# A fixed order for the prologue and the first eight weight units of a two-layer decoder trunk

## The chip, the cores and the metric

The kernel runs on one core of one Trainium2 chip. The metric is the device time of one execution in microseconds; less is better. It is given as the median of three executions, and a profile shows one more execution.

## What is computed

The reference is a decoder trunk of two layers on 256 positions of width 1024, all in float32. Each layer is a SwiGLU block, a mixer (Mamba-2 in the first layer, block-sparse attention in the second) and another SwiGLU block. Each of these six blocks works on a modulated norm of x, whose shift, scale and gate come from a product of SiLU(c) with a 1024 x 3072 matrix:

```python
def rmsnorm(x, g):
    y = xf * lax.rsqrt(jnp.mean(xf * xf, axis=-1, keepdims=True) + RMS_EPS)
    return (y * g).astype(x.dtype)

def modulate(x, g, c_act, w, b):
    m = c_act @ w + b
    shift, scale, gate = jnp.split(m, 3, axis=-1)
    return rmsnorm(x, g) * (1.0 + scale[:, None, :]) + shift[:, None, :], gate[:, None, :]

def swiglu(h, w_gate, w_up, w_down):
    return (jax.nn.silu(h @ w_gate) * (h @ w_up)) @ w_down

for i in range(DEPTH):
    h, g = modulate(x, norm_g[i, 0], c_act, mod_w[i, 0], mod_b[i, 0])
    x = x + 0.5 * g * swiglu(h, ffn_w_gate[i, 0], ffn_w_up[i, 0], ffn_w_down[i, 0])
    ...
```

## The kernel before

The weights stream through the core once. They are cut into units of 16 blocks of 128x128 (1 MB). A unit lands in one of three buffers `raw`, and is split into two halves of eight blocks. Of each half, ScalarE makes the high part (`hi`, a rounded copy, L309) and VectorE the low part (`lo`, raw minus `hi`, L316); there are six buffers of each, so three units. X, the modulated input, is split in the same way into XH and XL. TensorE then makes three matmuls of 256 columns per block (`prod`, L382 to L384): hi with XH, hi with XL, lo with XH. A unit is 48 matmuls.

The modulation vectors are made on VectorE. A block of 128 columns of the modulation matrix (`mraw`, 512 KB, five buffers) is multiplied by c, spread over all partitions in `cb`, and summed (`modulation`, L340); a small operation makes the vector's column of it (`vectors`, L325 and L327).

The prologue (L991 to L1025) loads c, the identity and x, spreads c over the partitions by eight transposes (L1011), squares x and adds the squares (L1014 to L1016), sums them over partitions by 16 instructions on TensorE (`rstd_sum`, L393), takes the root (L396) and makes the row `rb` (L406 to L408). The first eight units are the part of the first SwiGLU block that goes row block by row block: unit k needs only row block k of X. For each k VectorE makes two sums (scale block k, L327, and shift block k, L325), then u = x * scale * rb (L1032); ScalarE makes XH of it (L1035), VectorE XL (L1036). So unit k can begin as soon as its own two sums are there. All eight PSUM banks collect these eight units (L535 to L545). From unit 8 on a unit holds all row blocks of one output column, and its results are evacuated as they come.

The order of loads is a list (`LOADS`): for each of the first units scale block, shift block, weights. SP issues them in this order; `issue` (L272) goes on as long as a buffer of the list's next item is free, by the program's own count, and each load waits on the chip for the instruction that last reads its buffer. `pump` (L351) writes out splits and sums in the order of `ORDER`. In the prologue (`manual_schedule`) the program's order is kept; after it a scheduler sets the order of each engine's queue, by the buffers' dependencies and its own estimates. An engine works off its queue in order.

Of the kernel before, what the change touches and what calls it, by code (L numbers as in the profile page):

```python
# [146 lines left out]
def stream_order():  # L147


    items = []  # L150
    for j in range(6):
        for d in range(NK):
            items.append((j, 16 + d))
            if j < 5:
                items.append((j + 1, 8 + d))
        if j < 5:
            items += [(j + 1, d) for d in range(NK)]
    at = []
    for first, last, count in WINDOWS:
        at += [first + (last - first) * n / count for n in range(count)]  # L160
    assert len(at) == len(items) == 128
    order = []
    n = 0
    for i in range(len(ALL_UNITS)):
        if i < NK:
            order += [("m", 0, 8 + i)] * (i < 2) + [("m", 0, i)] + [("m", 0, 9 + i)] * (1 <= i < NK - 1)
        order.append(("w", i))
        while n < len(items) and at[n] <= i + 1:
            order.append(("m",) + items[n])
            n += 1  # L170
    assert n == len(items)
    return order
# [15 lines left out]
    pass  # L188


@with_exitstack
def hybrid_trunk(ctx, tc, w, mod, xt, vec, const, out, dbg=None):
    nc = tc.nc
    pool = ctx.enter_context(tc.tile_pool(name="main", bufs=1))
    psp = ctx.enter_context(tc.tile_pool(name="psum", bufs=1, space=bass.MemoryType.PSUM))
    mm, act, dve, gps = nc.tensor, nc.scalar, nc.vector, nc.gpsimd

    raw = [pool.tile([128, UW], F32, name=f"raw{i}") for i in range(N_RAW)]
    hi = [pool.tile([128, 128 * SUB], F32R, name=f"hi{i}") for i in range(N_SUB)]
# [12 lines left out]
    osel = pool.tile([128, 32], F32, name="osel")  # L212
    sel = pool.tile([128, 32], F32R, name="sel")
    b1 = pool.tile([128, 48], F32, name="b1")
    MV = pool.tile([128, 6, 3, NK], F32, name="MV")
    acc = pool.tile([128, 6, 24], F32, name="acc")
    ssq = pool.tile([128, L], F32, name="ssq")
# [8 lines left out]
    st = Core()  # L226
    st.bank = 0
    st.ut = 0
    st.sq = 0
# [32 lines left out]

    st.d = st.p = st.m = st.mdma = st.w = st.wdma = st.s = 0
    st.cur = -1
    st.on_mod = None
    st.sub = None
    st.known = set()
    st.hook = st.pending = None
    st.u = {}
    st.ahead = 2  # L270

    def issue(last=len(LOADS)):  # L272
# [32 lines left out]
    def split(q):  # L305
        i, half = SUBS[q]
        wd = 128 * SUB
        r, h, l = raw[i % N_RAW][:, half * wd:half * wd + wd], hi[q % N_SUB], lo[q % N_SUB]
        act.activation(h, r, AF.Copy)  # L309
        if st.pending:  # L310
            st.pending()
            st.pending = None
        c = wd * POOL_PART[PHASE_OF[i]] // 16
        if c:
            gps.tensor_sub(l[:, :c], r[:, :c], h[:, :c].bitcast(F32))
        ins = dve.tensor_sub(l[:, c:wd], r[:, c:wd], h[:, c:wd].bitcast(F32)).ins  # L316
        if i >= NK:
            st.sub = ins

    def vectors(j, kind, k0, k1):  # L320

        o, a = MV[:, j, kind, k0:k1], acc[:, j, 8 * kind + k0:8 * kind + k1]
        c = V_MB + 32 * j + 8 * kind
        if kind == 0:
            dve.tensor_add(o, a, V[:, c + k0:c + k1])  # L325
        elif kind == 1 and k1 == k0 + 1:
            dve.tensor_scalar(o, a, b1[:, 8 * j + k0:8 * j + k1], V[:, V_NG + 32 * j + k0:V_NG + 32 * j + k1],  # L327
                              op0=OP.add, op1=OP.mult)
# [6 lines left out]
        st.known |= {(j, 8 * kind + k) for k in range(k0, k1)}  # L335

    def modulation(j, c):
        kind, k = divmod(c, 8)
        one = j == 0 and kind < 2
        ins = dve.scalar_tensor_tensor(junk, mraw[SLOT["m", j, c]], 1.0, cb, op0=OP.mult, op1=OP.mult,  # L340
                                       accum_out=acc[:, j, c:c + 1]).ins
# [3 lines left out]
        st.m += 1  # L345
        if one or k == 7:
            vectors(j, kind, k if one else 0, k + 1)
        if st.on_mod:
            st.on_mod(j, c)

    def pump(q):  # L351

# [27 lines left out]
    def prod(ps, i, b, xh, xl, start, stop):  # L380
# [2 lines left out]
        mm.matmul(ps, h, xl, start=False, stop=False, skip_group_check=True)  # L383
        mm.matmul(ps, l, xh, start=False, stop=stop, skip_group_check=True)  # L384


    def rstd_sum(parts, n):

        ps = bank()
        c = (D, D_IN).index(n)  # L390
        for e, s in enumerate(parts):
            for t in range(2):
                mm.matmul(ps[:, t:t + 1], s[:, 128 * t:128 * t + 128], ones[:, c:c + 1], start=e == 0 and t == 0,  # L393
                          stop=e == len(parts) - 1, skip_group_check=True)
        q, r, t = (sm[:, 2 * i:2 * i + 2] for i in range(3))
        act.activation(q, ps[:, 0:2], AF.Sqrt, bias=eps)  # L396
# [104 lines left out]
    def ffn(j, p):  # L501
        i0 = BASE[p]
        with tc.tile_pool(name=f"ffn{p}", bufs=1) as fp:
# [30 lines left out]

            if p == 0:  # L535
                bs = [bank_pair() for _ in range(4)]
                for k in range(NK):
                    if k == 4:
                        preload(AF.Silu)
                    for m in range(8):  # L540
                        for s in range(2):
                            prod(bs[m // 2][:, m % 2, L * s:L * s + L], k, 2 * m + s, XH[:, k, :L], XL[:, k, :L],
                                 k == 0 and s == 0, k == NK - 1)
                        if k == NK - 1 and m % 2:
                            evac(m - 1, bs[m // 2])  # L545
                st.on_mod = None
# [444 lines left out]
    with tc.tile_pool(name="start", bufs=1) as sp:  # L991
        sq0 = sp.tile([128, NK, L], F32, name="sq0")
        ca = sp.tile([128, 8], F32, name="ca")
        xv = x.rearrange("p a b -> p (a b)")
        early = ExitStack()
# [29 lines left out]
    st.p = 2  # L1025

    def first_x(j, c):

        k = c % 8
        if c >= 8:  # L1030
            st.u[k] = utmp()
            dve.scalar_tensor_tensor(st.u[k], x[:, k, :], MV[:, j, 1, k:k + 1], rb, op0=OP.mult, op1=OP.mult)  # L1032
        else:
            S, u = MV[:, j, 0, k:k + 1], st.u[k]
            act.activation(XH[:, k, :L], u, AF.Identity, bias=S)  # L1035
            st.pending = lambda: dve.scalar_tensor_tensor(  # L1036
                XL[:, k, :L], u, S, XH[:, k, :L].bitcast(F32), op0=OP.add, op1=OP.subtract)

    first_x(0, 8)
    first_x(0, 0)  # L1040
    st.on_mod = first_x
    pump(0)
    early.close()
    ffn(0, 0)
    mamba(1, 1)
    ffn(2, 2)
# [90 lines left out]
```

## Time and profile before

| | us |
|---|---|
| median of three executions | 1115.83 (1115.04 to 1116.04) |
| the profiled execution | 1115.07 |
| its span, first to last instruction | 1113.3 |
| TensorE busy in it | 1090.7 |
| VectorE busy | 897.4 |
| ScalarE busy | 602.4 |

The rows further below come from this one execution. Its span is 1.8 us shorter than its time. A row of a timeline gives the start in us from the span's start, then the duration, then engine, line, operation and tiles. Matmuls are pipelined: one that is shown with 0.28 us begins 0.12 us after the one ahead of it. The share of the granted clock is recorded only from its first change on, so a stretch ahead of that prints as 1.00 whatever the clock was; the distance of the matmuls tells the level there.

### The profile page before, as it was taken

How to read it: one execution, taken by the hardware profiler on the slowest of the kernel's cores; microseconds unless marked ns; L12 is line 12 of the kernel's file. 1: busy time of each engine (PE TensorE's matmuls, PEld its weight loads, DVE VectorE, ACT ScalarE, POOL GpSimd, SP SyncE). 2: the span in 40 equal slices, each digit the busy share in tenths (PEclk: the TensorE clock that was granted, in tenths of full speed). 3: DMA queues.
4: the chain of work that ended last, by engine and by line, in shares of the span. 5: the costliest groups of instructions: out<-in, count | busy, mean ns of one | idle time of the engine just before them, and what ended most of it. 6: DMA issues, size and time to landing. Idle time of an engine off the chain costs nothing.

```text
span 1113.3 us, 22076 instructions
## 1 busy us (share of the span) xinstructions
PE 1090.7 (98%) x9050; PEld 1067.7 (96%) x9050; DVE 897.4 (81%) x1445; ACT 602.4 (54%) x919; POOL 55.4 (5%) x61
## 2 busy tenths in 40 slices
PE   6999999999999998999999999999999999999997
PEld 6999999999899998999999999999988899999996
DVE  6998989899899999999976889886697779555542
ACT  4463445676776657444544644454475666444541
POOL 0000001000000001000001000001211210000010
PEclk9999999999999999999999999999999999999998
DMA  9989988853444663899966499986544336555531
GB/s 349 381 335 369 352 319 302 301 200 117 175 166 142 240 238 128 302 356 367 375 246 246 160 346 334 356 308 263 186 174 156 121 115 222 190 184 183 186 136 39
DMA packets 50358, 269.00 MB, mean 242 GB/s; under 512 B 5840, under 2 KB 6608, under 8 KB 28624
## 3 DMA queue, kind: packets, MB, share of 16 engines
q1 hardware_dynamic: 50256, 267.58, 65.4%
q8 instruction: 71, 1.16, 0.4%
q14 instruction: 31, 0.25, 0.1%
HBM read 266.51 MB, written 1.05 MB: 240 GB/s over the span
## 4 chain that ended last, share of the span: by engine, by line
PE 94%; DVE 4%; ACT 1%; issue 1%; DMA 0%; SPq 0%; DVEq 0%; ACTq 0%
PE bank L383 29%; PE bank L382 29%; PE bank L384 29%; PE bank L734 1%; DVE lo L316 1%; PE bank L957 1%; PE bank L959 1%; PE bank L958 1%; PE bank L874 1%; PE bank L393 1%; PE bank L915 1%; DVE x L458 0%; ACT hi L309 0%; DMA x<-in_xt_dram 0%; DVE X L439 0%
## 5 line engine op out<-in xcount | busy, mean ns | idle before, releaser
L316 DVE TENSOR_TENSOR lo<-raw,hi 128x1024 fp32r<-128x1024 f32 x361 | 437.7, 1221 | 136.9 <-ACT hi L309 136.6
L309 ACT ACTIVATE hi<-raw 128x1024 fp32r<-128x1024 f32 x361 | 376.8, 1057 | 310.8 <-PE bank L383 253.2
L383 PE MATMUL bank<-X,hi 128*128 128x256 f32 (+1 forms) x1928 | 542.7, 282 | 1.5 <-DVE X L439 1.4
L382 PE MATMUL bank<-X,hi 128*128 128x256 f32 (+1 forms) x1928 | 538.3, 282 | 4.0 <-ACT hi L309 2.5
L384 PE MATMUL bank<-X,lo 128*128 128x256 f32 (+1 forms) x1928 | 538.8, 281 | 0.2 <-DVE lo L316 0.2
L382 PEld LDWEIGHTS bank<-X,hi 128*128 128x128 f32 x1928 | 364.2, 190 | 8.6 <-issue 3.4
L383 PEld LDWEIGHTS bank<-X,hi 128*128 128x128 f32 x1928 | 363.7, 189 | 2.8 <-DVE X L439 1.8
L384 PEld LDWEIGHTS bank<-X,lo 128*128 128x128 f32 x1928 | 363.4, 189 | 0.4 <-DVE lo L316 0.4
L384 PE MATMUL bank<-H,lo 128*128 128x256 f32 x704 | 196.9, 280 | 0.0
L382 PE MATMUL bank<-H,hi 128*128 128x256 f32 x704 | 196.3, 279 | 0.0
L383 PE MATMUL bank<-H,hi 128*128 128x256 f32 x704 | 196.2, 279 | 0.0
L340 DVE SCALAR_TENSOR_TENSOR junk<-mraw,cb 128x1024 bf16<-128x1024 f32 x144 | 175.4, 1218 | 0.9 <-DMA mraw<-in_mod_dram 0.2
L383 PEld LDWEIGHTS bank<-H,hi 128*128 128x128 f32 x704 | 132.3, 188 | 0.0
L384 PEld LDWEIGHTS bank<-H,lo 128*128 128x128 f32 x704 | 132.1, 188 | 0.0
L382 PEld LDWEIGHTS bank<-H,hi 128*128 128x128 f32 x704 | 131.6, 187 | 0.0
L416 POOL TENSOR_TENSOR ssq<-ssq,sq 128x256 f32<-128x256 f32 x36 | 34.4, 955 | 966.3 <-ACT sq L414 965.8
L522 ACT ACTIVATE sg<-bank 128x512 f32<-128x512 f32 x41 | 24.0, 585 | 38.9 <-PE bank L384 38.9
L634 DVE SCALAR_TENSOR_TENSOR cv<-bank,V,cv 128x255 f32<-128x255 f32 (+2 forms) x96 | 44.3, 474 | 0.5
L458 DVE SCALAR_TENSOR_TENSOR x<-bank,MV,x 128x256 f32<-128x256 f32 x40 | 19.1, 480 | 29.2 <-PE bank L384 29.1
L414 ACT ACTIVATE sq<-x 128x256 f32<-128x256 f32 x36 | 14.9, 414 | 50.6 <-DVE x L458 45.9
L382 PE MATMUL bank<-GH,hi 128*128 128x256 f32 x128 | 36.2, 284 | 1.1 <-DVE cv L634 0.9
L384 PE MATMUL bank<-GH,lo 128*128 128x256 f32 x128 | 36.0, 282 | 0.0
(179 smaller groups left out, 924.1 us busy)
## 6 DMA issues: line engine op xcount, KB each, us to landing
raw<-in_w_dram SPq DMA_DIRECT2D x169, 1024.0 KB, 5.1
mraw<-in_mod_dram SPq DMA_DIRECT2D x144, 512.0 KB, 6.5
raw<-in_w_dram SPq DMA_DIRECT2D x23, 512.0 KB, 8.1
x<-in_xt_dram SPq DMA_DIRECT2D x2, 512.0 KB, 4.6
out_dram<-x SPq DMA_DIRECT2D x3, 256.0 KB, 2.3
out_dram<-x SPq DMA_DIRECT2D x2, 128.0 KB, 1.9
V<-in_vec_dram SPq DMA_DIRECT2D x1, 196.5 KB, 8.3
mask<-in_const_dram SPq DMA_DIRECT2D x1, 192.0 KB, 8.1
```

The source lines that it names most:

```text
L309: act.activation(h, r, AF.Copy)
L316: ins = dve.tensor_sub(l[:, c:wd], r[:, c:wd], h[:, c:wd].bitcast(F32)).ins
L340: ins = dve.scalar_tensor_tensor(junk, mraw[SLOT["m", j, c]], 1.0, cb, op0=OP.mult, op1=OP.mult, accum_out=acc[:, j, c:c + 1]).ins
L382: mm.matmul(ps, h, xh, start=start, stop=False, skip_group_check=True)
L383: mm.matmul(ps, h, xl, start=False, stop=False, skip_group_check=True)
L384: mm.matmul(ps, l, xh, start=False, stop=stop, skip_group_check=True)
L393: mm.matmul(ps[:, t:t + 1], s[:, 128 * t:128 * t + 128], ones[:, c:c + 1], start=e == 0 and t == 0, stop=e == len(parts) - 1, skip_group_c ...
L414: act.activation(s, src, AF.Square)
L416: gps.tensor_add(total, total, s)
L458: dve.scalar_tensor_tensor(x[:, d, :], ps, g, x[:, d, :], op0=OP.mult, op1=OP.add)
L522: act.activation(s, ps[:, :, :L], AF.Silu)
L634: dve.scalar_tensor_tensor(o[:, c, s:], ps[:, c, :L - s], V[:, wc + 3 - s:wc + 4 - s], o[:, c, s:], op0=OP.mult, op1=OP.add)
```

## The change

The prologue and the first eight units are written in a fixed order. `Pinned` wraps TensorE, ScalarE and VectorE: while `st.pin` is set, each instruction is told to keep its place in program order among those that are told so too. `manual_schedule` is gone.

The identity is made on POOL (a memset and a select) instead of loaded. The squares are added once more, so that each half of x gives one part to sum over partitions instead of two. Between the steps of the prologue TensorE makes 22 transposes of the identity into a bank that nobody reads (`warm`). The small vector operations go to ScalarE (`first_vector`), the first u reads the rows from PSUM, and the high half of unit 0 is written ahead of the vectors. In `first_units` VectorE alternates low halves, X and sums in a written order, and TensorE goes through a half unit in three passes of eight matmuls (`sweeps`) instead of three matmuls per block. In the loop's last round `st.pin` is taken off, and `pump` writes out the two halves of unit 8 ahead of the last unit's matmuls.

```diff
         if i < NK:
-            order += [("m", 0, 8 + i)] * (i < 2) + [("m", 0, i)] + [("m", 0, 9 + i)] * (1 <= i < NK - 1)
+            order += [("m", 0, 8 + i), ("m", 0, i)]
...
+class Pinned:
+    def __init__(self, tc, engine, st):
+        self.tc, self.engine, self.st = tc, engine, st
+    def __getattr__(self, name):
+        f = getattr(self.engine, name)
+        def call(*args, **kw):
+            ins = f(*args, **kw)
+            if self.st.pin:
+                self.tc.keep_in_program_order(ins)
+            return ins
+        return call
...
-    mm, act, dve, gps = nc.tensor, nc.scalar, nc.vector, nc.gpsimd
+    st = Core()
+    st.pin = False
+    mm, act, dve = (Pinned(tc, e, st) for e in (nc.tensor, nc.scalar, nc.vector))
+    gps = nc.gpsimd
...
+    def sweeps(q, outs, xh, xl, start, stop):
+        h, l = hi[q % N_SUB], lo[q % N_SUB]
+        for a, b, first, last in ((h, xh, start, False), (h, xl, False, False), (l, xh, False, stop)):
+            for n, ps in enumerate(outs):
+                mm.matmul(ps, a[:, 128 * n:128 * n + 128], b, start=first and n % 2 == 0, stop=last, skip_group_check=True)
...
-        early.enter_context(tc.manual_schedule())
+        st.pin = True
         nc.sync.dma_start(V[:, :V_MB + 32], vec[:, :V_MB + 32])
-        nc.sync.dma_start(ident, const[:, 0:128])
...
+        gps.memset(ident, 1.0)
+        gps.affine_select(ident, ident, [[-1, 128]], OP.is_equal, 0.0, base=0, channel_multiplier=1)
...
+        preload(AF.Sqrt, False)
         dve.tensor_scalar(b1[:, :8], V[:, V_MB + 8:V_MB + 16], 1.0, None, op0=OP.add)
+        dve.tensor_mul(b1g, b1[:, :8], V[:, V_NG:V_NG + 8])
         pc = [bank(), bank()]
+        idle, ps, pr = bank(), bank(), bank()
+        def warm(n):
+            for _ in range(n):
+                mm.transpose(idle[:, :128], ident, ident)
         for k in range(NK):
             mm.transpose(pc[k // 4][:, 128 * (k % 4):128 * (k % 4) + 128], ca[:, k:k + 1].to_broadcast([128, 128]), ident)
+        warm(6)
+        act.activation(cb[:, :512], pc[0], AF.Copy)
         for h in range(2):
             c = 4 * h
             act.activation(sq0[:, c:c + 2, :], x[:, c:c + 2, :], AF.Square)
             dve.tensor_mul(sq0[:, c + 2:c + 4, :], x[:, c + 2:c + 4, :], x[:, c + 2:c + 4, :])
             dve.tensor_add(sq0[:, c:c + 2], sq0[:, c:c + 2], sq0[:, c + 2:c + 4])
+            dve.tensor_add(sq0[:, c], sq0[:, c], sq0[:, c + 1])
             if h == 0:
-                for q in range(2):
-                    act.activation(cb[:, 512 * q:512 * q + 512], pc[q], AF.Copy)
-        preload(AF.Sqrt, False)
-        modulation(*ORDER[0][1:])
-        r = rstd_sum([sq0[:, c, :] for c in (0, 1, 4, 5)], D)
-        modulation(*ORDER[1][1:])
-        rstd_rows(r, True)
+                act.activation(cb[:, 512:], pc[1], AF.Copy)
+            for t in range(2):
+                mm.matmul(ps[:, t:t + 1], sq0[:, c, 128 * t:128 * t + 128], ones[:, 0:1], start=h == 0 and t == 0,
+                          stop=h == 1, skip_group_check=True)
+            warm((4, 3)[h])
+        root(ps)
...
+        columns_sum(0, 8)
+        first_vector(8)
+        r = rstd(ps)
+        columns_sum(0, 0)
+        for t in range(2):
+            mm.transpose(pr[:, 128 * t:128 * t + 128], r[:, t:t + 1].to_broadcast([128, 128]), ident)
+        warm(9)
+        high(0)
+        first_u(0, pr[:, :L])
+        first_vector(0)
+        first_x(0)
+        act.activation(rb, pr[:, :L], AF.Copy)
+    def first_units(bs, evac):
+        for k in range(NK):
+            issue()
+            last = k == NK - 1
+            low(2 * k)
+            dve.scalar_tensor_tensor(XL[:, k, :L], ut[k % 3], MV[:, 0, 0, k:k + 1], XH[:, k, :L].bitcast(F32),
+                                     op0=OP.add, op1=OP.subtract)
+            high(2 * k + 1)
+            if not last:
+                columns_sum(0, 9 + k)
+                first_vector(9 + k)
+                high(2 * k + 2)
+            low(2 * k + 1)
+            st.w += 1
+            if not last:
+                first_u(k + 1, rb)
+                columns_sum(0, k + 1)
+                first_vector(k + 1)
+                first_x(k + 1)
+            issue()
+            if k == 4:
+                preload(AF.Silu)
+            if last:
+                st.pin = False
+                st.p, st.s = 3 * NK, 2 * NK
+                pump(2 * NK + 1)
+            for q in range(2):
+                st.pin = True
+                sweeps(2 * k + q, [bs[m // 2][:, m % 2, L * s:L * s + L] for m in range(4 * q, 4 * q + 4) for s in range(2)],
+                       XH[:, k, :L], XL[:, k, :L], k == 0, last)
+                if last:
+                    st.pin = False
+                    evac(4 * q, bs[2 * q])
+                    evac(4 * q + 2, bs[2 * q + 1])
```

At two places the order of the engines' queues is shown, first before and then in the changed program. A number behind a name is its buffer: unit i uses buffer i modulo 3 of `raw`, and of `hi` and `lo` buffers 0 and 1, 2 and 3 or 4 and 5. In the changed program L201, the line of the wrapper, stands for every instruction of the three engines.

The first place is VectorE's queue around unit 6, which has buffers 0 and 1 of `lo`; unit 7 has 2 and 3, unit 8 has 4 and 5 and `raw2`. Before (the sums and small vectors between unit 6 and unit 7 are left out):

```order
L316 TENSOR_TENSOR lo0_70<-raw0_61,hi0_64 128x1024
L1036 SCALAR_TENSOR_TENSOR X_83<-ut0_99,MV_93,X_83 128x256
L316 TENSOR_TENSOR lo1_71<-raw0_61,hi1_65 128x1024
L316 TENSOR_TENSOR lo2_72<-raw1_62,hi2_66 128x1024
L1036 SCALAR_TENSOR_TENSOR X_83<-ut1_100,MV_93,X_83 128x256
L316 TENSOR_TENSOR lo3_73<-raw1_62,hi3_67 128x1024
L523 TENSOR_TENSOR hh0_187<-sg0_185,bank_106 128x512
L316 TENSOR_TENSOR lo4_74<-raw2_63,hi4_68 128x1024
```

The same engine in the changed program, from the second low half of unit 5 on:

```order
L201 TENSOR_TENSOR lo5_75<-raw2_63,hi5_69 128x1024
L201 SCALAR_TENSOR_TENSOR ut0_100<-x_82,MV_94,rb_103 128x256
L201 SCALAR_TENSOR_TENSOR junk_81,acc_95<-mraw3_79,cb_84 128x1024
L201 TENSOR_TENSOR lo4_74<-raw2_63,hi4_68 128x1024
L201 TENSOR_TENSOR lo5_75<-raw2_63,hi5_69 128x1024
L201 TENSOR_SCALAR b1_92<-V_85 128x40
L201 TENSOR_TENSOR lo0_70<-raw0_61,hi0_64 128x1024
L201 SCALAR_TENSOR_TENSOR X_83<-ut0_100,MV_94,X_83 128x256
```

The low halves of unit 8 (the second pair with `raw2`) and the add on the late part of V have moved from behind unit 7 to ahead of unit 6's first low half and its X.

The second place is TensorE's queue from the transposes of c to unit 0. Before:

```order
L1011 MATMUL bank<-ident,ca 128x128 x8
L393 MATMUL bank<-ones,sq_110 128x1 x8
L406 MATMUL bank<-ident,sm 128x128 x2
L382 MATMUL bank<-X,hi_64 128x256
L383 MATMUL bank<-X,hi_64 128x256
```

In the changed program:

```order
L201 MATMUL bank<-ident,ca 128x128 x8
L201 MATMUL bank<-ident 128x128 x6
L201 MATMUL bank<-ones,sq_111 128x1 x2
L201 MATMUL bank<-ident 128x128 x4
L201 MATMUL bank<-ones,sq_111 128x1 x2
L201 MATMUL bank<-ident 128x128 x3
L201 MATMUL bank<-ident,sm 128x128 x2
L201 MATMUL bank<-ident 128x128 x9
L201 MATMUL bank<-X,hi_64 128x256 x16
L201 MATMUL bank<-X,lo_70 128x256 x8
```

Four of the eight sums over partitions are gone, the transposes of the identity stand between the steps, and a half unit goes by passes. SP's queue is the same in the first eight units but for the identity, which is gone; behind unit 8's load, unit 11's now stands ahead of unit 9's.

## Rows read from the trace of the kernel before

**Rows 1.** The page's chain of waits, by engine.

```profile
PE 94%; DVE 4%; ACT 1%; issue 1%; DMA 0%; SPq 0%; DVEq 0%; ACTq 0%
```

**Rows 2.** Busy us by stretch, then clock, DMA share, GB/s.

```profile
0.00:50.00 50.00, 40.66 (x294) 39.84 (x295) 41.47 (x77) 23.18 (x32) 0.40 (x8) 1.00 0.96 362
100.00:150.00 50.00, 50.00 (x427) 50.00 (x427) 45.98 (x66) 25.86 (x32) 0.00 (x0) 1.00 0.92 355
```

**Rows 3.** TensorE's longest wait, 15 to 75 us: total, times, longest.

```profile
PE bank L382 <- ACT hi L309: 2.5, 1, 2.5
```

**Rows 4.** The chain in order of time, 9 to 16 us.

```profile
11.12 0.27 ACT sm L396
...
14.51 0.96 ACT hi L309
...
15.51 0.58 PE bank L382
```

**Rows 5.** Busy us by stretch, columns as in rows 2.

```profile
15.50:21.60 6.10, 6.09 (x29) 6.09 (x30) 6.06 (x10) 2.61 (x4) 0.00 (x0) 1.00 1.02 410
24.00:29.66 5.66, 5.66 (x50) 5.66 (x49) 5.62 (x11) 1.93 (x3) 0.00 (x0) 1.00 1.03 408
```

**Rows 6.** TensorE's timeline: the rows that open units 6 and 7.

```profile
52.40 0.76 PE L382 MATMUL bank<-X,hi 128*128 128x256 f32 x5
...
58.12 0.75 PE L382 MATMUL bank<-X,hi 128*128 128x256 f32 x5
```

**Rows 7.** SP's timeline at the start.

```profile
1.16 0.42 SPq L998 DMA_DIRECT2D ident<-in_const_dram  x1
1.63 0.42 SPq L1000 DMA_DIRECT2D x<-in_xt_dram  x1
```

**Rows 8.** A group up to 15.5 us: busy us, mean ns | idle before.

```profile
L393 PE MATMUL bank<-ones,sq 128*128 128x1 f32 x16 | 3.5, 352 | 1.5 <-DVE sq L1016 1.5
```

**Rows 9.** VectorE's timeline, units 5 to 8.

```profile
45.70 1.23 DVE L316 TENSOR_TENSOR lo<-raw,hi 128x1024 fp32r<-128x1024 f32 x1
...
54.12 1.22 DVE L340 SCALAR_TENSOR_TENSOR junk<-mraw,cb 128x1024 bf16<-128x1024 f32 x1
...
55.26 0.48 DVE L1032 SCALAR_TENSOR_TENSOR ut<-x,MV,rb 128x256 f32<-128x256 f32 x1
...
55.73 1.22 DVE L316 TENSOR_TENSOR lo<-raw,hi 128x1024 fp32r<-128x1024 f32 x1
56.86 0.48 DVE L1036 SCALAR_TENSOR_TENSOR X<-ut,MV,X 128x256 fp32r<-128x256 f32 x1
57.34 1.23 DVE L316 TENSOR_TENSOR lo<-raw,hi 128x1024 fp32r<-128x1024 f32 x1
...
63.41 0.19 DVE L302 TENSOR_SCALAR b<-V 128x40 f32<-128x40 f32 x1
63.51 0.68 DVE L523 TENSOR_TENSOR hh<-sg,bank 128x512 f32<-128x512 f32 x1
```

**Rows 10.** SP's timeline at two loads.

```profile
42.29 0.33 SPq L292 DMA_DIRECT2D mraw<-in_mod_dram  x1
...
46.96 0.33 SPq L285 DMA_DIRECT2D raw<-in_w_dram  x1
```

**Rows 11.** Those loads, us to landing; last, the page's median.

```profile
mraw<-in_mod_dram SPq DMA_DIRECT2D x1, 512.0 KB, 5.7
raw<-in_w_dram SPq DMA_DIRECT2D x1, 1024.0 KB, 7.4
...
raw<-in_w_dram SPq DMA_DIRECT2D x169, 1024.0 KB, 5.1
```

**Rows 12.** TensorE's last dense matmul, and the stretch behind it.

```profile
1103.34 0.28 PE L384 MATMUL bank<-H,lo 128*128 128x256 f32 x1
...
1107.00:1113.30 6.30, 0.00 (x0) 0.00 (x0) 2.56 (x5) 0.31 (x1) 0.00 (x0) 0.50 0.46 166
```

**Rows 13.** A group of POOL over the whole execution.

```profile
L869 POOL TENSOR_SCALAR bh<-dist 128x384 f32<-128x384 f32 x16 | 20.3, 1273 | 71.0 <-DVE am L880 64.8 <-PE bank L384 5.6
```

More of the change, by code (lines that the diff above doesn't have):

```diff
@@ L214, in hybrid_trunk @@
     b1 = pool.tile([128, 48], F32, name="b1")
+    b1g = pool.tile([128, NK], F32, name="b1g")
     MV = pool.tile([128, 6, 3, NK], F32, name="MV")
@@ L225, in hybrid_trunk @@
     psum = psp.tile([128, 8, 512], F32, name="bank")
-    st = Core()
     st.bank = 0
@@ L264, in hybrid_trunk @@
     st.cur = -1
-    st.on_mod = None
     st.sub = None
     st.known = set()
-    st.hook = st.pending = None
-    st.u = {}
+    st.hook = None
     st.ahead = 2
@@ L309, in split @@
         act.activation(h, r, AF.Copy)
-        if st.pending:
-            st.pending()
-            st.pending = None
         c = wd * POOL_PART[PHASE_OF[i]] // 16
@@ L325, in vectors @@
             dve.tensor_add(o, a, V[:, c + k0:c + k1])
-        elif kind == 1 and k1 == k0 + 1:
-            dve.tensor_scalar(o, a, b1[:, 8 * j + k0:8 * j + k1], V[:, V_NG + 32 * j + k0:V_NG + 32 * j + k1],
-                              op0=OP.add, op1=OP.mult)
         elif kind == 1:
@@ L335, in vectors, with columns_sum @@
         st.known |= {(j, 8 * kind + k) for k in range(k0, k1)}
+    def columns_sum(j, c):
+        ins = dve.scalar_tensor_tensor(junk, mraw[SLOT["m", j, c]], 1.0, cb, op0=OP.mult, op1=OP.mult,
+                                       accum_out=acc[:, j, c:c + 1]).ins
+        st.m += 1
+        return ins
     def modulation(j, c):
         kind, k = divmod(c, 8)
-        one = j == 0 and kind < 2
-        ins = dve.scalar_tensor_tensor(junk, mraw[SLOT["m", j, c]], 1.0, cb, op0=OP.mult, op1=OP.mult,
-                                       accum_out=acc[:, j, c:c + 1]).ins
+        ins = columns_sum(j, c)
         if st.sub:
@@ L344, in modulation @@
                 mybir.DependencyClass.NoSync, mybir.DependencyReason.DATA), reason="not before the splits that it follows")
[L345 to L349, printed above, removed]
+        if k == 7:
+            vectors(j, kind, 0, 8)
     def pump(q):
@@ L395, in rstd_sum, with root, rstd @@
         q, r, t = (sm[:, 2 * i:2 * i + 2] for i in range(3))
-        act.activation(q, ps[:, 0:2], AF.Sqrt, bias=eps)
+        root(ps)
+        return rstd(ps)
+    def root(ps):
+        act.activation(sm[:, 0:2], ps[:, 0:2], AF.Sqrt, bias=eps)
+    def rstd(ps):
+        q, r, t = (sm[:, 2 * i:2 * i + 2] for i in range(3))
         dve.reciprocal(r, q)
@@ L536, in ffn @@
                 bs = [bank_pair() for _ in range(4)]
[L537 to L546, printed above, removed]
+                first_units(bs, evac)
                 m0 = i0 + 8
@@ L994, in hybrid_trunk @@
         xv = x.rearrange("p a b -> p (a b)")
-        early = ExitStack()
-        early.enter_context(tc.manual_schedule())
+        st.pin = True
         nc.sync.dma_start(V[:, :V_MB + 32], vec[:, :V_MB + 32])
-        nc.sync.dma_start(ident, const[:, 0:128])
         for h in range(2):
@@ L1016, in hybrid_trunk @@
             dve.tensor_add(sq0[:, c:c + 2], sq0[:, c:c + 2], sq0[:, c + 2:c + 4])
+            dve.tensor_add(sq0[:, c], sq0[:, c], sq0[:, c + 1])
             if h == 0:
-                for q in range(2):
-                    act.activation(cb[:, 512 * q:512 * q + 512], pc[q], AF.Copy)
-        preload(AF.Sqrt, False)
-        modulation(*ORDER[0][1:])
-        r = rstd_sum([sq0[:, c, :] for c in (0, 1, 4, 5)], D)
-        modulation(*ORDER[1][1:])
-        rstd_rows(r, True)
[L1025 to L1043, printed above, removed]
+                act.activation(cb[:, 512:], pc[1], AF.Copy)
[3 more added lines that the diff above has]
+            warm((4, 3)[h])
+        root(ps)
+        def first_vector(c):
+            k = c % 8
+            o, a = MV[:, 0, c // 8, k:k + 1], acc[:, 0, c:c + 1]
+            if c < 8:
+                act.activation(o, a, AF.Identity, bias=V[:, V_MB + c:V_MB + c + 1])
+            else:
+                act.activation(o, a, AF.Identity, scale=V[:, V_NG + k:V_NG + k + 1], bias=b1g[:, k:k + 1])
@@ new lines, in first_u, with first_x, high, low @@
+        def first_u(k, row):
+            dve.scalar_tensor_tensor(ut[k % 3], x[:, k, :], MV[:, 0, 1, k:k + 1], row, op0=OP.mult, op1=OP.mult)
+        def first_x(k):
+            act.activation(XH[:, k, :L], ut[k % 3], AF.Identity, bias=MV[:, 0, 0, k:k + 1])
+        def high(q):
+            i, half = SUBS[q]
+            act.activation(hi[q % N_SUB], raw[i % N_RAW][:, 1024 * half:1024 * half + 1024], AF.Copy)
+        def low(q):
+            i, half = SUBS[q]
+            dve.tensor_sub(lo[q % N_SUB], raw[i % N_RAW][:, 1024 * half:1024 * half + 1024], hi[q % N_SUB].bitcast(F32))
@@ new lines, in hybrid_trunk @@
+        columns_sum(0, 8)
[44 more added lines that the diff above has]
+                    evac(4 * q + 2, bs[2 * q + 1])
+        st.known |= {(0, c) for c in range(16)}
```

## The prediction

> **What bounds the kernel now.** I read the chain of waits first, then the busy time by stretch, then TensorE's own waits, then the timelines of the first 65 us. TensorE holds 94% of the chain [rows 1]. In the first 50 us it is busy for 40.66 us, from 100 us on for 50 of 50 [rows 2]. So the time is a start, and then a stream of matmuls that almost nothing holds up: between 15 and 75 us TensorE's one long wait is 2.5 us, for the high half that opens unit 0 [rows 3]. Whatever moves the instant at which unit 8 begins (the first unit that the change leaves alone) moves the end by as much. From there on the matmuls stand in the same order in both programs but for small swaps. I therefore predict that instant.
>
> Before, unit 0 begins at 15.51 us, behind the root at 11.12 and the first high half at 14.51 [rows 4]. Up to 21.6 us TensorE gets through 29 matmuls in 6.1 us [rows 5], 0.21 us for each; later one unit, 48 matmuls, takes 5.72 us, from 52.40 to 58.12 [rows 6], 0.119 for each: the lower of the clock's two levels (1.2 GHz), then the higher (2.4 GHz). Unit 8 begins at 58.12 + 5.7 = 63.8 us.
>
> **The start, part by part.** The identity no longer goes through SP's queue, so the loads behind it are issued 0.47 us earlier (1.63 less 1.16 [rows 7]). The 16 sum matmuls took 3.5 us [rows 8]; half are gone, and of the 8 left only 4 (0.9 us) follow the last add. The added adds cost VectorE about 0.35 us each, half of the 0.68 for 128x512 [rows 9], one of them exposed. The root comes about 1.2 us earlier, near 9.9. From there to X little changes: the copy of the rows is bypassed, the vectors go to ScalarE. The first high half, 1.0 us to its successor [rows 4], now runs ahead of X instead of behind it. So unit 0 begins at 15.5 - 1.2 - 1.0 - 0.1 = 13.2 us, or at 13.5 if the idle transposes run at the lower clock, since 9 of the 22 stand directly ahead of it: a gain of 2.0 to 2.3 us.
>
> VectorE then needs per unit two sums, two low halves, u and X's low part: 4 x 1.14 + 0.47 + 0.48 = 5.5 us, against 5.82 before (45.70 to 57.34 are two units) and TensorE's 5.7 [rows 9]. Up to unit 5 it stays ahead. Passes instead of triples are the same 48 matmuls: I cost them at nothing, since the weight loads are as many and stay beside them.
>
> **Where the gain goes.** VectorE's queue, shown above, has the two low halves of unit 8 in front of those of unit 6, and an engine works its queue in order. Unit 8's low halves need unit 8's weights, and that load goes into the buffer of unit 5: before, it was issued at 46.96 us, right behind unit 5's second low half, which began at 45.70 and took 1.23 [rows 9, 10]. In the changed program it waits for the same instruction. So its landing stands ahead of unit 6's low halves, of unit 6's X low part, and of all that TensorE does after the first eight matmuls of unit 6.
>
> When does it land? Unit 5's second low half ends at 46.93 less the start's 2.3 us, 44.6, or up to 1.5 us sooner, as five units take 0.3 less each; the load is issued then, at 43.1 to 44.6. It doesn't land soon, for the queue ahead of it is full: data arrive at 408 GB/s with all DMA engines busy [rows 5], 512 KB in 1.28 us. Before, the last block for unit 7's sums was issued at 42.29 and landed 5.7 us later, at 47.99 [rows 10, 11]; behind it come the two halves of unit 7 and the 1 MB of unit 8, four times 512 KB. That gives 47.99 - 0.47 + 4 x 1.28 = **52.6 us**. Bounds: 48.2 at the earliest, 43.1 and the 5.1 us that a load of this size takes in the median of the kernel [rows 11]; 53.9 at the latest, as before: 46.96 + 7.4 - 0.47 [rows 10, 11]. I take 52.6, nearest to what the stream did.
>
> From the landing to TensorE: a high half on ScalarE 1.0, two low halves at 1.13, the add on the constants V, which stands there too, 0.10 (63.41 to 63.51), unit 6's first low half 1.13, X's low part 0.48 [rows 4, 9], and some hand-overs of 0.05: 5.2 us. TensorE goes on at 52.6 + 5.2 = **57.8 us**. The first eight matmuls of unit 6 are done by 48 to 51 us, according to the clock at the start, so it idles for 7 to 10 us. How early it gets there doesn't matter: the gain of the start is spent waiting, all of it.
>
> Then 40 matmuls of unit 6 and 48 of unit 7 are left: 88 x 0.119 = 10.4 us. And the clock falls in so long a pause: at the end of the kernel the last dense matmul begins at 1103.34, and from 1107.00 on the granted clock is 0.50, which is 1.2 GHz [rows 12]. The price of the restart is that of the start: 29 matmuls, each 0.21 - 0.119 us too long, 2.7 us [rows 5, 6]. That is one sample; the bounds are 0 and about 3, and I take the row. The other producers keep ahead meanwhile: unit 6's second low half is ready a sum and a low half (2.3 us) after the restart, X of unit 7 about 4.6 us after it.
>
> Sum: unit 8 at 57.8 + 10.4 + 2.7 = 70.9 us, against 63.8: **+7.1 us**. The profiled execution took 1115.07 us, with a span of 1113.3, and lies 0.76 under the median of 1115.83; on its own time the forecast is **1122.2 us**. After unit 8 I cost nothing: units 9 to 11 load while TensorE idles and works off units 6 and 7. If that cover were gone, unit 9's load, which is now queued behind unit 11's, would show as a wait in unit 9.
>
> **One operation without a row.** The identity needs a select on POOL. The nearest row is POOL's own, 1.27 us for 128x384 [rows 13]; that would put it near 2.5 us, before the activated c, at no cost. The other end is that it comes so late that ScalarE's first copy of c, now ahead of the squares, holds these; that begins at about 4.4 us.
>
> **Rivals.** (a) *The identity comes late.* If it comes three such rows (3.8 us) after 4.4, VectorE's whole chain shifts by 3.8 and the load's issue with it, to 46.9 to 48.4; with the 7.4 us that it took before [rows 11] it lands near 55.0 in place of 52.6: 1122.2 + 2.4 = 1124.6. For it: no row shows POOL with such an instruction. Against it: all of POOL's rows are short. Chance 0.16. The Trainium skill (GPSIMD Engine Reference, section 2.1) says that the first call to a freshly loaded POOL routine pays about 6 us for loading its code; by that rule the identity would be there near 8 us, as in this rival. No run here shows it.
>
> (b) *Faster: unit 8's load is no obstacle.* TensorE loses nothing if X's low part of unit 6 is there by 48.2, that is if the load lands by 43.0. Then the start's 2.3 us are kept, and 2.7 more if the idle transposes bring the clock up early: 1115.07 - 5.0 = 1110.1, or 1112.8 without the clock. Against it: the load can't even be issued before 43.1. Chance 0.05. The Trainium skill (TensorE: Matmul & The Clock Gate, Part 4) says that transposes don't count for the clock as other work does; by that this rival gives 1112.8 and the main sum stays, because the pause takes the clock away in any case.
>
> (c) *About as before.* The load lands near its lower bound: 48.2 + 5.2 + 10.4 = 63.8 us, which is 1115.1 without the clock's price and 1117.8 with it. For it: the load is issued some 3 us earlier than before. Against it: the queue is full. Chance 0.10.
>
> **The numbers.** The forecast has the remaining 0.69. Its own width is the landing (2 us less to 1.3 more) and the clock (2 us less to nothing more): 1118 to 1123.5. Rival (a) reaches above that; I end at 1124.5, which leaves out (b), most of (c) and a part of (a), 2 in 10 at most. A measurement of this kernel tells about 0.2%, 2.2 us, from no change. Faster by more than that: 0.05, rival (b). Within it: 0.11, rival (c) and the lowest edge of the forecast. Slower: 0.84.
>
> **What would show it.** In the profile of the changed kernel: unit 0 begins near 13.2 to 13.5 us; TensorE has one wait of 6 to 10 us in its first 70, for X's low part on VectorE, after eight matmuls of unit 6; VectorE idles at the same time for the high half of unit 8, and ScalarE for the DMA of unit 8's weights, which is issued near 44 and lands near 52 to 53; the matmuls behind the wait are 0.21 us apart at first; from 75 us on TensorE is busy without a gap. I am wrong if TensorE's longest wait there is under 3 us, if it ends on anything but unit 8's load, or if the matmuls after it are 0.12 us apart at once.

## The result, and the profile of the kernel after

The kernel after takes 1127.57 us in the median (four executions, 1126.32 to 1128.87) against 1115.53 before: a ratio of 1.0111, interval 1.0099 to 1.0122, **12.0 us slower**. The forecast was 1122.2, with a range that ends at 1124.5: the side was right, the size was not.

The rows below are of an execution that took 1128.87 us (span 1127.2). First TensorE's waits between 12 and 75 us (total, times, longest), of which the longest before was 2.5 [rows 3]:

```profile
PE bank L201 <- DVE X L201: 7.9, 1, 7.9
```

Then the page's chain by engine, where PE was 94% [rows 1]:

```profile
PE 90%; DMA 4%; DVE 3%; ACT 2%; issue 1%; SPq 0%; DVEq 0%; ACTq 0%
```

The wait stands where it was forecast. Timelines of TensorE, ScalarE, VectorE and SP around it:

```profile
13.57 0.56 PE L201 MATMUL bank<-X,hi 128*128 128x256 f32 x1
...
57.39 2.08 PE L201 MATMUL bank<-X,hi 128*128 128x256 f32 x8 [7.91 <-DVE X L201]
...
10.14 0.26 ACT L201 ACTIVATE sm<-bank,eps 128x2 f32<-128x2 f32 x1 [2.96 <-PE bank L201]
...
52.25 2.00 ACT L201 ACTIVATE hi<-raw 128x1024 fp32r<-128x1024 f32 x2 [4.36 <-DMA raw<-in_w_dram]
...
53.34 2.36 DVE L201 TENSOR_TENSOR lo<-raw,hi 128x1024 fp32r<-128x1024 f32 x2 [7.27 <-ACT hi L201]
55.61 0.19 DVE L201 TENSOR_SCALAR b<-V 128x40 f32<-128x40 f32 x1
55.72 1.22 DVE L201 TENSOR_TENSOR lo<-raw,hi 128x1024 fp32r<-128x1024 f32 x1
56.85 0.48 DVE L201 SCALAR_TENSOR_TENSOR X<-ut,MV,X 128x256 fp32r<-128x256 f32 x1
...
44.55 0.33 SPq L303 DMA_DIRECT2D raw<-in_w_dram  x1
...
45.41 0.42 SPq L316 DMA_DIRECT2D V<-in_vec_dram  x1
```

Read from below: unit 8's load is issued at 44.55, the second load of V behind it at 45.41. VectorE stands still until unit 8's high halves are there, makes its two low halves, then b from V, and only then unit 6's low half and X's low part, which TensorE waits for. The forecast was of the instant at which unit 8 begins. Its first matmul in TensorE's timeline, in the kernel after and then before:

```profile
70.28 0.40 PE L201 MATMUL bank<-X,hi 128*128 128x256 f32 x2
```

```profile
63.74 0.28 PE L382 MATMUL bank<-X,hi 128*128 128x256 f32 x1
```

That is +6.5, where +7.1 was forecast. At the first matmul on H it is +6.1 (149.41 against 143.36). From there to the last matmul on H the kernel after takes 967.7 us and the kernel before 960.0: 7.7 more, in a stretch where I had cost nothing. These are the windows of two down-projections (matmuls on H alone), of the kernel before and then of the kernel after; the columns are those of [rows 2], cut down to TensorE.

```profile
165.00:200.00 35.00, 35.00 (x299) 1.00 0.83 306
570.00:605.00 35.00, 35.00 (x299) 1.00 0.76 281
```

```profile
165.00:200.00 35.00, 35.00 (x294) 1.00 0.79 285
570.00:605.00 35.00, 35.00 (x294) 1.00 0.74 270
```

A window counts every matmul under way in it, and one lasts 0.28 us, so the spacing is (35 + 0.28) / count: 118.0 ns before, 120.0 after, with TensorE busy and the clock at 1.00 throughout. A count is good to one matmul. More exact is a whole down-projection, 528 such matmuls: from its first start to its last it takes 62.07 us before and 63.23 after, in each of the four, which is 117.8 ns and 120.0. Four times 1.16 is 4.6 us. TensorE's order is the same there. The 576 matmuls on GH, GL, OH and OL, the same kind of operand in the two mixers, also come 2 to 3 ns later, 1.2 to 1.5 us in all.

A third, small piece is a fall of the clock in the middle of the kernel. Busy time is the same before and after, but this execution has a granted clock of 0.97 and 13 matmuls less (1.5 us):

```profile
400.00:452.00 52.00, 48.84 (x394) 1.00 0.49 169
```

```profile
400.00:452.00 52.00, 48.85 (x381) 0.97 0.52 184
```

### The profile page after: what moved, and what is told of

Same layout as the page of the kernel before. It is cut to its first block, busy times and chain, and to the rows that moved or that the text cites. A ratio compares the mean times of both kernels' runs of the same rounds, so it can differ in the third digit from the quotient of the medians.

```text
span 1127.2 us, 22154 instructions
## 1 busy us (share of the span) xinstructions
PE 1101.6 (98%) x9064; PEld 1078.6 (96%) x9064; DVE 896.1 (80%) x1432; ACT 611.0 (54%) x935; POOL 55.6 (5%) x63
## 3 DMA queue, kind: packets, MB, share of 16 engines
q8 instruction: 71, 1.16, 0.4%
## 4 chain that ended last, share of the span: by engine, by line
PE 90%; DMA 4%; DVE 3%; ACT 2%; issue 1%; SPq 0%; DVEq 0%; ACTq 0%
PE bank L201 90%; DMA raw<-in_w_dram 4%; DVE lo L201 1%; ACT hi L201 1%; DVE x L201 1%; DVE X L201 0%; DVE ut L201 0%; ACT wt L201 0%; DVE cv L201 0%; ACT th L201 0%; DVE wt L201 0%; SPq L310 0%; DVE xs L201 0%; ACT L201 0%; SPq L303 0%
## 5 line engine op out<-in xcount | busy, mean ns | idle before, releaser
L201 PE MATMUL bank<-X,hi 128*128 128x256 f32 (+1 forms) x3856 | 683.4, 283 | 10.9 <-DVE X L201 9.3
L201 PEld LDWEIGHTS bank<-X,hi 128*128 128x128 f32 x3856 | 586.8, 190 | 16.7 <-DVE X L201 10.8
L201 ACT ACTIVATE hi<-raw 128x1024 fp32r<-128x1024 f32 x361 | 380.7, 1059 | 372.0 <-PE bank L201 305.3
L201 DVE TENSOR_TENSOR lo<-raw,hi 128x1024 fp32r<-128x1024 f32 x361 | 439.4, 1222 | 156.4 <-ACT hi L201 156.3
L201 PE MATMUL bank<-X,lo 128*128 128x256 f32 (+1 forms) x1928 | 523.1, 281 | 0.0
L201 PEld LDWEIGHTS bank<-X,lo 128*128 128x128 f32 x1928 | 356.4, 189 | 0.0
L201 PE MATMUL bank<-H,hi 128*128 128x256 f32 x1408 | 253.6, 281 | 0.0
L201 PEld LDWEIGHTS bank<-H,hi 128*128 128x128 f32 x1408 | 218.2, 189 | 0.0
L201 PE MATMUL bank<-H,lo 128*128 128x256 f32 x704 | 199.2, 283 | 0.0
L201 DVE SCALAR_TENSOR_TENSOR junk<-mraw,cb 128x1024 bf16<-128x1024 f32 x144 | 175.4, 1218 | 0.9 <-DMA mraw<-in_mod_dram 0.3
L201 PEld LDWEIGHTS bank<-H,lo 128*128 128x128 f32 x704 | 131.6, 187 | 0.0
L201 DVE SCALAR_TENSOR_TENSOR cv<-bank,V,cv 128x255 f32<-128x255 f32 (+2 forms) x96 | 44.5, 476 | 0.5
L201 DVE SCALAR_TENSOR_TENSOR x<-bank,MV,x 128x256 f32<-128x256 f32 x40 | 19.1, 481 | 28.7 <-PE bank L201 28.7
L201 PE MATMUL bank<-GH,hi 128*128 128x256 f32 x128 | 36.5, 287 | 1.2 <-DVE cv L201 0.9
L201 PE MATMUL bank<-GH,lo 128*128 128x256 f32 x128 | 36.4, 285 | 0.0
L201 PE MATMUL bank<-GL,hi 128*128 128x256 f32 x128 | 36.1, 282 | 0.0
L201 ACT ACTIVATE sq<-x 128x256 f32<-128x256 f32 (+1 forms) x38 | 16.1, 425 | 33.9 <-DVE x L201 32.4
L201 ACT ACTIVATE H<-hh 128x512 fp32r<-128x512 f32 (+1 forms) x47 | 27.7, 592 | 11.0 <-DVE hh L201 11.0
L201 DVE SCALAR_TENSOR_TENSOR X<-x,MV,X 128x256 fp32r<-128x256 f32 x40 | 28.5, 714 | 5.8 <-ACT X L201 5.8
L201 DVE TENSOR_TENSOR hh<-sg,bank 128x512 f32<-128x512 f32 x41 | 27.8, 681 | 4.1 <-ACT sg L201 4.0
L201 DVE TENSOR_TENSOR H<-hh,H 128x512 fp32r<-128x512 f32 (+1 forms) x47 | 30.5, 651 | 0.4 <-ACT H L201 0.3
```

The costliest lines, as they stand in the source:

```text
L201: ins = f(*args, **kw)
```

## The experiments

Medians of the kernel before that was run beside them: 1115.2 to 1115.7.

### Where H lies: 32 bytes more, in the kernel before

The change declares one new tile, `b1g`, 32 bytes a partition, ahead of MV and of all that the blocks' own pools hold. Theory A: that move alone slows the matmuls on H. The kernel before, with nothing but the move:

```diff
-    b1 = pool.tile([128, 48], F32, name="b1")
+    b1 = pool.tile([128, 56], F32, name="b1")[:, :48]
```

> The kernel before, with b1 declared 8 columns wider (32 bytes a partition) and used as before: every instruction stands in the same order on every engine, and only the tiles that are declared behind b1, H, GH, GL, OH and OL among them, start 32 bytes later, as they do in the kernel after. Theory A (the down-projections' matmuls are slower in the kernel after because H lies 32 bytes further on): 4 to 6 us slower than the kernel before, 1119.5 to 1121.5, matmuls on H at about 120 ns instead of 117.8, the start unchanged. Rival B (they are slower because the other engines' work and the transfers fall at other moments beside them): no change, 1115.5 within 1.

Measured: 1120.05 us, ratio 1.005 (1.0038 to 1.0063), 4.8 us slower. The window of the first block:

```profile
165.00:200.00 35.00, 35.00 (x294) 1.00 0.82 302
```

So 294 and not 299: theory A holds, for the order of TensorE's instructions and of SP's loads is untouched. **32 bytes in a declaration cost 4.8 us.** In this profile the first matmul on H comes 1.4 us sooner than before (141.98 against 143.36), and from it to the last it is 966.0 us against 960.0, so the move itself costs about 6. It moves everything declared behind b1, and no run moves H with nothing else. The second run gave b1g 64 bytes, in the kernel after:

```diff
-    b1g = pool.tile([128, NK], F32, name="b1g")
+    b1g = pool.tile([128, 2 * NK], F32, name="b1g")[:, :NK]
```

> The kernel after, with b1g declared 16 columns wide (64 bytes a partition) and 8 of them used: the order of all instructions is that of the kernel after, H and the others move 32 bytes more. Theory A (32 bytes do it, and 64 don't): 4 to 6.5 us faster than the kernel after, 1121 to 1123.5, and a window in mid down-projection (550:600) shows about 426 matmuls instead of 422. Rival B: no change, 1127.5 within 1.5. In both the wait of 7.9 us ahead of unit 6 stays.

Measured: 1126.05 us (1.0105, 1.0092 to 1.0119), 1.5 us under the kernel after with intervals that overlap, and the same 294 matmuls in the window. Theory A's guess that 64 bytes are as good as none is a miss: both starts are slow ones.

### The stall: which instruction holds unit 6 up

I had blamed unit 8's splits. This run keeps them behind units 6 and 7:

```diff
-                st.pin = False
                 st.p, st.s = 3 * NK, 2 * NK
                 pump(2 * NK + 1)
+                st.pin = False
```

> The kernel after, with the splits of unit 8 kept in program order behind those of units 6 and 7 on ScalarE and VectorE. Theory C (TensorE's wait of 7.9 us ahead of unit 6, and the lost clock behind it, come from the place of unit 8's splits in the two queues alone): the wait goes, unit 8 begins at about 60 instead of 70.9, and the time falls by 8 to 11 us, 1116.5 to 1119.5; the matmuls on H stay slow. Rival D (the late load of unit 8 is the cause, and the wait only moves to unit 8): under 3 us faster, 1124.5 to 1127.5.

> Both edits to the kernel after: unit 8's splits in their place, and b1g 64 bytes wide. If theories A and C hold and add up: 1111 to 1114, faster than the kernel before by 2 to 4.5 us. Under B: as the run with the order alone. Under D: 1118 to 1122.

Measured: 1125.91 (1.0095, 1.0079 to 1.011) and, with 64 bytes as well, 1124.76 us (1.0092). Theory C falls: 1.7 us, not 8 to 11. Nor is it rival D, though the first time lies in its range, for the wait (5.5 us) still stands ahead of unit 6. VectorE's timeline of the first of the two shows what I had overlooked:

```profile
53.50 0.20 DVE L201 TENSOR_SCALAR b<-V 128x40 f32<-128x40 f32 x1 [7.78 <-DMA V<-in_vec_dram]
53.62 1.21 DVE L201 TENSOR_TENSOR lo<-raw,hi 128x1024 fp32r<-128x1024 f32 x1
54.75 0.48 DVE L201 SCALAR_TENSOR_TENSOR X<-ut,MV,X 128x256 fp32r<-128x256 f32 x1
```

With unit 8's splits gone the add that makes b from V waits by itself. Its load is issued from `issue`, in the middle of the fixed order, and `constants` writes the add right there; with `st.pin` set it may not slide back. ScalarE's copy `sel` waited likewise, 6.6 us for osel, but ScalarE then stood still for 2.0 us more, for VectorE's next sum, so the add was the later of the two:

```profile
54.16 0.23 ACT L201 ACTIVATE sel<-osel 128x32 fp32r<-128x32 f32 x1 [6.62 <-DMA osel<-in_const_dram]
56.40 0.39 ACT L201 ACTIVATE MV<-acc,b1g,V 128x1 f32<-128x1 f32 x1 [2.01 <-DVE junk L201]
```

The next two runs move both behind unit 8's splits; the second has b1g at 256 bytes too.

```diff
     def constants():
...
-        dve.tensor_scalar(b1[:, 8:].rearrange("p (a b) -> p a b", a=5),
...
                 pump(2 * NK + 1)
+                dve.tensor_scalar(b1[:, 8:].rearrange("p (a b) -> p a b", a=5),
...
                 st.pin = False
...
-                act.activation(sel, osel, AF.Copy)
+                tc.keep_in_program_order(act.activation(sel, osel, AF.Copy))
```

```diff
-    b1g = pool.tile([128, NK], F32, name="b1g")
+    b1g = pool.tile([128, 64], F32, name="b1g")[:, :NK]
```

> The run with unit 8's splits in their place, and in addition the two instructions that wait for the second load of vectors and constants (VectorE's sum into b1 from V, ScalarE's copy osel to sel) kept behind unit 8's splits. Theory C2 (two kinds of work that wait for a late transfer stood ahead of unit 6's low half, unit 8's splits and these; either alone holds TensorE up): the wait of 5.5 us goes, at most 2 us of it is left, the first gate copy of unit 7 comes at 57 to 60 instead of 65.7, and the time is 1116.5 to 1119.5, 6 to 9 us below the run before it. Rival E (the pace of the transfers holds unit 6 up, whatever the order): 1124 to 1126.

> As the run named free, and b1g declared 64 columns wide (256 bytes a partition, 8 columns used), so that H stands at the same place modulo 256 bytes as in the kernel before. Theory A2 (the spacing of matmuls on H is set by its start address modulo 256 bytes or a part of it; 0 and 32 more than the kernel before differ, and 64 more is slow too): matmuls on H back at 117.8 ns, 4.5 to 5 us below the run named free, 1111.5 to 1114.5. Rival (only the address of the kernel before itself is fast, by a longer period or by its distance to something else): as the run named free.

Measured: 1118.15 us (1.0028, 1.0016 to 1.0039) and 1111.89 us (0.9972, 0.9961 to 0.9984). TensorE's longest wait between 12 and 75 us is now 0.8 us, and it is busy from 14 to 60 us throughout, 389 matmuls (308 in the kernel after, 352 before), here with 256 bytes:

```profile
14.00:60.00 46.00, 46.00 (x389) 1.00 1.03 410
```

Rival E (the transfers' pace) is out. With 256 bytes the window on H is back at 299, as in the kernel before.

Were there two causes, or did the one bring the other? One run moves only the constants' add (and `sel`), and leaves unit 8's splits to the scheduler:

```diff
...
                 st.pin = False
                 st.p, st.s = 3 * NK, 2 * NK
                 pump(2 * NK + 1)
+                st.pin = True
+                dve.tensor_scalar(b1[:, 8:].rearrange("p (a b) -> p a b", a=5),
...
+                st.pin = False
```

> The kernel after with one edit alone: VectorE's sum into b1 from the second load of V is pinned behind unit 7's low halves instead of inside the fixed order ahead of unit 6's (and ScalarE's copy osel to sel is kept in program order); unit 8's splits are left to the scheduler, which then puts them behind unit 7's by itself. Theory G (the pinned sum is the one cause: it waits for a transfer queued behind unit 8's load, and unit 8's splits had only been put ahead of it because the scheduler saw unit 6 held up): as the run named free, 1117 to 1119.5. Rival C2 (two separate causes): 1123 to 1126.

Measured: 1118.32 us (1.0026, 1.0018 to 1.0035), the same as with both edits. Theory G holds: unit 8's splits are no second cause. The edit moves `sel` with the add, so what `sel` alone would cost isn't shown; TensorE's wait was for X on VectorE, where the add stood. Freed of it, the scheduler puts unit 8's splits behind unit 7's by itself. VectorE's timeline shows units 6 and 7 follow without a wait for a transfer:

```profile
50.89 1.22 DVE L201 TENSOR_TENSOR lo<-raw,hi 128x1024 fp32r<-128x1024 f32 x1
52.02 0.48 DVE L201 SCALAR_TENSOR_TENSOR X<-ut,MV,X 128x256 fp32r<-128x256 f32 x1
52.82 1.23 DVE L201 TENSOR_TENSOR lo<-raw,hi 128x1024 fp32r<-128x1024 f32 x1 [0.32 <-ACT hi L201]
```

### The idle transposes

```diff
-            for _ in range(n):
+            for _ in range(0):
                 mm.transpose(idle[:, :128], ident, ident)
```

> As the run named free with 256 bytes, without the 22 idle transposes on TensorE. If the idle transposes bring the granted clock up early: the clock rises 5 to 8 us after unit 0 begins instead of within 2 us of it, the first 6 us have about 29 matmuls instead of 50, and the time is 1 to 2.5 us more. If transposes do not raise the clock (the rule of the Trainium skill): the clock rises at the same moment as with them, and the time is the same within 0.7.

Measured: 1113.13 us (0.9979, 0.997 to 0.9988), 1.2 us more than with them, between medians whose intervals overlap. In the two profiles unit 0 begins at 13.0 us, and the first matmul on H at 139.5 us with them and 141.1 without. TensorE's windows after unit 0's begin, with them and without:

```profile
13.60:16.00 2.40, 2.40 (x18) 1.00 1.02 413
16.00:18.40 2.40, 2.40 (x23) 1.00 1.04 420
```

```profile
13.60:16.00 2.40, 2.40 (x13) 1.00 1.03 410
16.00:18.40 2.40, 2.40 (x14) 1.00 1.04 422
18.40:20.80 2.40, 2.40 (x23) 1.00 1.02 411
```

Fourteen matmuls in 2.4 us is the lower level of the clock, 23 the higher one: with the transposes the spacing falls from 0.21 to 0.12 us at 14.8 us, without them at 18.2, 3.4 us later. The Trainium skill (TensorE: Matmul & The Clock Gate, Part 4) says that transposes don't count for the clock as other work does; in these two runs 22 of them, of float32, bring it up sooner. The page speaks of a transpose mode of TensorE; the trace doesn't show whether these ran in it.

### How far the address of H reaches

The kernel before with H moved inside its own pool, by another distance in each block:

```diff
-            H = fp.tile([128, NM, 2, L], F32R, name="H")
+            gap = {0: 24, 2: 32, 3: 48, 5: 64}[p]
+            H = fp.tile([128, gap + NM * 2 * L], F32R, name="H")[:, gap:].rearrange("p (a b c) -> p a b c", a=NM, b=2)
```

> The kernel before with H moved within its own pool, by 96, 128, 192 and 256 bytes in the four feed-forward blocks in turn. Read is the spacing of the matmuls on H in each block. Theory A2: the block moved by 256 bytes shows 117.8 as before; the others show which part of the address counts: if 128 bytes are the period, the block moved by 128 shows 117.8 too. Rival: none of the four is at 117.8.

One execution took 1113.86 us. Windows in its four blocks:

```profile
165.00:200.00 35.00, 35.00 (x300) 1.00 0.80 302
570.00:605.00 35.00, 35.00 (x311) 1.00 0.75 276
760.00:790.00 30.00, 30.00 (x252) 1.00 0.56 196
1060.00:1090.00 30.00, 30.00 (x258) 1.00 0.32 106
```

From the first start of each block to its last, 96 bytes give 117.3 ns, 128 give **113.3**, 192 give 120.0, and 256 give 117.8, as in place. The place before was neither the worst nor the best. The tiles declared behind H in its pool move with it here, so the move isn't H's quite alone; H is the one of them that these matmuls read. So b1g at 128 bytes, in the run with the freed constants:

```diff
-    b1g = pool.tile([128, NK], F32, name="b1g")
+    b1g = pool.tile([128, 32], F32, name="b1g")[:, :NK]
```

> The run named free with b1g 32 columns wide (128 bytes a partition), so that H, GH, GL, OH and OL start 64 bytes past a multiple of 256, as H did in the block moved by 128 bytes, whose matmuls came at 113.3 ns. Theory A2 (start address modulo 256 sets the spacing in every block): about 113.3 ns in all four down-projections, 2112 x 4.44 ns = 9.4 us below the run with 256 bytes, 1101.5 to 1104. Rival (the third block alone can be fast): 1109 to 1111.

Measured: **1103.81 us**, ratio 0.9896 (0.9881 to 0.9911): the version that beats both, 11.9 us under the kernel before and 23.8 under the one after. All four blocks are fast, at 113.3 ns; two of them (the first ends inside its window):

```profile
165.00:200.00 35.00, 35.00 (x309) 1.00 0.78 291
570.00:605.00 35.00, 35.00 (x311) 1.00 0.75 279
```

Against the run with 256 bytes it gains 8.1 of the 9.4 us expected.

I then moved the slices of X too, with H at what should be the same place modulo 256 bytes (by the declared sizes; the runs record no addresses):

```diff
-    X = pool.tile([128, NK, 2, L + 2], F32R, name="X")
-    XH, XL = X[:, :, 0, :], X[:, :, 1, :]
+    X = pool.tile([128, 42 + 48 + 2 * NK * (L + 2)], F32R, name="X")
+    XH, XL = (X[:, n:n + NK * (L + 2)].rearrange("p (a b) -> p a b", a=NK) for n in (42, 42 + NK * (L + 2) + 48))
...
-    b1g = pool.tile([128, NK], F32, name="b1g")
...
+    b1g = sm[:, 6:14]
```

> The run named free with b1g put into unused columns of sm and X laid out as eight XH, a gap, eight XL, so that slice k of either starts at 40 + 8k bytes past a multiple of 256 (before: 128 + 16k and 136 + 16k), and H 64 bytes past one. Theory A3 (the same rule holds for matmuls on X: slow at 128 and at 0, fast about 64): X's 5640 or so matmuls come at 113.5 to 117 ns instead of 118.2, 1074 to 1097. Rival (X's spacing is set by something else): within 1 us of the run with H at 64.

Measured: 1119.33 us (1.0029, 1.002 to 1.0037), a miss on both theories: 15.5 us more than without that layout. The matmuls on H were slow again, at 117.8 ns, which is 9.4 us:

```profile
165.00:200.00 35.00, 35.00 (x300) 1.00 0.76 287
```

So were those on X themselves, here in a stretch that holds nothing else, without the layout and with it:

```profile
80.00:130.00 50.00, 50.00 (x428) 1.00 0.94 362
```

```profile
80.00:130.00 50.00, 50.00 (x422) 1.00 0.95 357
```

Over the whole kernel their mean spacing goes from 118.1 to 119.3 ns, which is 6 to 7 us for 5880 of them; with the 9.4 that accounts for the difference. In the other runs X stays at 118.1 to 118.3, wherever H lies.

A last run asks whether 256 bytes is the period at all. It is the scan again, with gaps of 96, 160, 288 and 544 columns.

> The kernel before with H moved within its own pool by 384, 640, 1152 and 2176 bytes in the four feed-forward blocks in turn; 128 bytes gave 113.3 ns a matmul, and 384 bytes gave 117.8 in the run in which X was laid out anew as well. Theory A4 (the period is 512 bytes or a divisor of 1024 or 2048 above 256): the first block shows 117.8, and the fourth 113.3; the second shows 113.3 if 512 is the period, the third if 1024 is. Rival (the period is 256 and the new layout of X took the speed away): all four show 113.3. Rival (distance to other tiles counts, no period): mixed, the fourth not at 113.3.

One execution took 1105.62 us, against 1115.3 before on the same chip. Its four blocks:

```profile
165.00:200.00 35.00, 35.00 (x311) 1.00 0.80 309
570.00:605.00 35.00, 35.00 (x311) 1.00 0.77 276
760.00:790.00 30.00, 30.00 (x267) 1.00 0.53 191
1060.00:1090.00 30.00, 30.00 (x267) 1.00 0.17 67
```

All are at 113.3, as the rival with a period of 256 bytes had it: as long as the rest lies still, the start of H counts modulo 256 bytes in every distance tried. But the first block should have H where the run with the new layout had it, by the declared sizes, and there it was slow. If that count is right, H's own address isn't all, and the place of something that moved with X counts for it too. What the rule is stays open.

## Why the prediction was wrong

**How the 12.0 us come about.** The pinned add (with `sel`) costs 9.3 (1127.57 less 1118.32), the 256 bytes, which put H and what lies behind it back in place, are worth 6.3 (1118.15 less 1111.89), and what is left of the change, the earlier start and the earlier clock, gains 3.5 (1111.89 against 1115.43). These are differences of medians, each good to about 1 us, and the falls of the clock in mid-kernel are in them. The traces agree: the start is 6.1 us late at the first matmul on H, and the matmuls on H and in the mixers lose another 5.8 to 6.1.

**Right, by its steps.** Unit 0 begins at 13.57 (forecast 13.2 to 13.5), behind a root at 10.14 (9.9). Unit 8's load is issued at 44.55 (43.1 to 44.6); its high halves begin at 52.25 (landing 52.6). TensorE waits 7.9 us (7 to 10) and goes on at 57.39 (57.8). Behind that the clock is low:

```profile
57.00:60.00 3.00, 2.61 (x12) 0.50 0.85 333
60.00:63.00 3.00, 3.00 (x17) 0.54 0.78 240
```

29 matmuls in 5.6 us, where 29 x 0.119 is 3.5: a price of 2.1 us (2.7). Unit 8 begins at 70.28 (70.9), 6.5 us later than before (7.1).

**Right in size, wrong in cause.** "the add on the constants V, which stands there too, 0.10": I had the row in hand and charged its duration alone. Its own load stands behind unit 8's in SP's queue, so it would have held VectorE until 53.5 without any of unit 8's splits. That they stood there was a consequence of it. The figure survived by luck: unit 8's high halves began at 52.25 in the one run, the add at 53.50 in the other, 1.3 us apart.

**Rival (a), the identity late.** Out: the select runs at 1.17 us.

```profile
1.17 0.29 POOL L1019 TENSOR_SCALAR_AFFINE_SELECT ident<-ident 128x128 f32<-128x128 f32 x1
```

The Trainium skill (GPSIMD Engine Reference, section 2.1) puts about 6 us on the first call of a freshly loaded POOL routine; this select, 1.17 us into the span, shows no such delay.

**The step that failed:** "After unit 8 I cost nothing." I looked there for loads that come late, and took equal instructions in equal order for equal time: the term was put at nothing. The new tile b1g, whose use stands in the diff shown, moved H and its like, and each of 2112 matmuls came 2.2 ns later: 4.6 us, with the mixers' matmuls about 6, and 1.5 more in the profiled execution for the clock. The signs of being wrong that were named all look at the first 75 us, and none of them showed. Rivals (b) and (c) had that gap too, and unit 8's load landed near 52.2, not by 43.0 or 48.2.

**The clock in mid-kernel.** TensorE stands still for 3.2 us in all between 400 and 452 us in every profile here. In five of fourteen the granted clock of that stretch is 0.97, which costs some 13 matmuls or 1.5 us. The executions of the kernel after lie near 1126.3 or 1128.8, and only one at 1128.87 has a profile, so whether this fall makes that difference isn't shown. What decides it is open.

## What to carry to other kernels

An instruction inside a fixed order costs what it waits for, not what it takes: go through the list and ask of each row where in its queue the last load it needs stands, the tiny ones first. A new tile moves every tile that is declared behind it, so compare the spacing of matmuls in stretches that the change doesn't touch; if it differs, the address is a suspect that one edit of a declaration can test. Where matmuls fill the time, trying a few starts for the moving operand is cheap: here 128 bytes were worth 8 us, and a new layout of X took them back and more.

## What the hardware showed that I had not expected

With clock, order and TensorE's busy share the same, matmuls of one shape on H came every 113.3, 117.3 to 117.8 or 120.0 ns on average, by where H lay (with what moved along), and in a run with one place for H all four blocks agreed. And 22 idle float32 transposes brought the clock up 3.4 us sooner.
